# Closing the other rows between the last expert's matmuls, with its down projection in unsplit fp32

## The chip, the cores and the metric

The kernel runs on one core of a Trainium2 chip. The metric is the device time of one execution in microseconds (us). The engines are TensorE (PE; its weight loads are PEld), VectorE (DVE), ScalarE (ACT), GpSimd (POOL) and SyncE (SP); DMA queues carry data between HBM and the on-chip memory.

## What is computed

One layer of a hybrid attention and recurrence backbone. Only its last part matters here, the expert-choice mixture of 16 experts over 1024 tokens of width 1024, each expert taking 128 tokens, and the norm and gated residual after it:

```python
aff = softmax(einsum("btd,de->bte", h, w_router))
top_aff, top_idx = top_k(swapaxes(aff, 1, 2), cap)            # cap = 128
xin = h[top_idx]
g = einsum("becd,edf->becf", xin, w_gate)
u = einsum("becd,edf->becf", xin, w_up)
y = einsum("becf,efd->becd", silu(g) * u, w_down) * top_aff[..., None]
f_lat = zeros((t, d)).at[idx].add(y)
x_lat = x_lat + gt2 * rmsnorm(f_lat, norm_post_ffn)
```

All arrays are fp32.

## The kernel before

Experts run one after the other. Each has 24 weight pieces of 128 x 1024 fp32 (512 KB): 16 for gate and up (two halves of 512 columns, four pieces each of gate and up in turn) and 8 for the down projection, one for each block of 128 hidden features. The pieces are loaded by SyncE (`fetch_to`, lines 1211 to 1221) into a ring of 36 buffers (`ring`, line 1186), far ahead. Two pieces ahead of use (`LEAD`, `take`, lines 1652 to 1657) each is split (`split_piece`, line 1391): ScalarE casts it to a rounded high part (line 1395), VectorE subtracts to get the low part (line 1396). Each product is then three matmuls in the rounded format: high by high, low by high, high by low (lines 1545 to 1547 and 1634 to 1636). The activations are transposed on TensorE and split in the same way (`split_T`, line 1521).

`gate_up` (line 1534) makes one half of the hidden features: 48 matmuls into two accumulators, then tanh on ScalarE and two products on VectorE (lines 1549 to 1551). `hid_T` (line 1554) transposes that half. `down` (line 1625) runs 48 matmuls into `y`. Experts 0 to 14 scale `y` and add it by a GpSimd scatter into `fd` (line 1643), a buffer in HBM that holds the sum over experts.

`out` already holds the residual rows. After expert 14, `bulk` (line 1565) loads the gain row `g2` and the eight 128-row blocks of `fd` into ring buffers, and gathers the last expert's own rows of `fd` and of the residual (line 1578). The closure that it returns, run after the last expert's matmuls (line 1639), closes the rows: a square with a row sum for each block on ScalarE (line 1586), a root for each pair of blocks (`rstd_of`, line 103: one VectorE instruction, line 105, and one GpSimd power, line 106), a scaling by root and gain on VectorE (line 1594), and a store by GpSimd's DMA queue that adds into `out` (line 1595). `fixup` (line 1607) then adds the last expert's `y` to its gathered rows, takes their norm and overwrites those rows of `out` by a scatter (line 1620), which has to come after the eight adding stores.

Instructions go out in each engine's order. For the last expert (`MAN = 1`, line 1673) the order on TensorE, VectorE, ScalarE and GpSimd is that of the program text; before it a planner orders them, and it always orders SyncE's loads. `bulk()` itself is called after expert 14's down projection, still under the planner.

## Time and profile before

| | us |
|---|---|
| median of 3 runs | 1549.85 (1548.72 to 1551.9) |
| the profiled execution | 1549.72 |
| its span in the trace | 1547.8 |
| TensorE busy in it | 1451.9 (94%) |
| VectorE busy | 1165.9 (75%) |
| ScalarE busy | 880.5 (57%) |
| GpSimd busy | 128.8 (8%) |

Times in the views count from the start of the span. Busy time is time in which an engine executes; a stretch in which TensorE is idle is seen in the timeline or in the windows. A matmul's recorded duration runs to its modelled end, so matmuls that follow each other overlap in the records, and the distance between starts tells their pace. A row of the timeline merges like instructions (x2, x3), with the idle time before it and what ended that.

### The profile page before, as it was taken

How to read it: one execution, taken by the hardware profiler on the slowest of the kernel's cores; microseconds unless marked ns; L12 is line 12 of the kernel's file. 1: busy time of each engine (PE TensorE's matmuls, PEld its weight loads, DVE VectorE, ACT ScalarE, POOL GpSimd, SP SyncE). 2: the span in 40 equal slices, each digit the busy share in tenths (PEclk: the TensorE clock that was granted, in tenths of full speed). 3: DMA queues.
4: the chain of work that ended last, by engine and by line, in shares of the span. 5: the costliest groups of instructions: out<-in, count | busy, mean ns of one | idle time of the engine just before them, and what ended most of it. 6: DMA issues, size and time to landing. Idle time of an engine off the chain costs nothing. (4 is left out here: it accounts for less than half of the span.)

```text
span 1547.8 us, 23432 instructions
## 1 busy us (share of the span) xinstructions
PE 1451.9 (94%) x8905; PEld 1198.4 (77%) x8905; DVE 1165.9 (75%) x1588; ACT 880.5 (57%) x1350; POOL 128.8 (8%) x139
## 2 busy tenths in 40 slices
PE   5999999999999988999999979999999999999990
PEld 1988988888978777999978736888888888888870
DVE  2628472849177768999945587999999999999983
ACT  2733443444211117988843315888888888888881
POOL 2100000000000001111000000111111111100003
PEclk9999999999999998999999999999999999999995
DMA  9210010111156616335036886999999999999836
GB/s 337 83 55 29 28 28 28 29 32 39 30 176 194 180 51 167 78 75 150 27 123 243 278 313 233 379 378 383 383 383 372 384 385 384 385 383 383 315 122 149
DMA packets 159308, 316.28 MB, mean 204 GB/s; under 512 B 13790, under 2 KB 50870, under 8 KB 159196
## 3 DMA queue, kind: packets, MB, share of 16 engines
q1 hardware_dynamic: 148592, 277.99, 49.8%
q0 software_dynamic: 9408, 33.54, 9.2%
q10 hardware_dynamic: 1196, 3.26, 0.6%
q8 instruction: 70, 1.15, 0.3%
q14 instruction: 42, 0.34, 0.1%
HBM read 274.36 MB, written 29.38 MB: 196 GB/s over the span
## 5 line engine op out<-in xcount | busy, mean ns | idle before, releaser
L1396 DVE TENSOR_TENSOR mlo<-mraw,mhi 128x1024 fp32r<-128x1024 f32 x340 | 407.5, 1222 | 18.1 <-ACT mhi L1395 13.8
L1395 ACT CAST mhi<-mraw 128x1024 fp32r<-128x1024 f32 x340 | 356.8, 1051 | 79.7 <-PE g L1546 28.2
L166 PE MATMUL pp<-h_hi,whi 128*128 128x512 f32 (+1 forms) x480 | 180.0, 375 | 0.0
L167 PE MATMUL pp<-h_lo,whi 128*128 128x512 f32 (+1 forms) x480 | 178.3, 371 | 0.0
L168 PE MATMUL pp<-h_hi,wlo 128*128 128x512 f32 (+1 forms) x480 | 178.0, 371 | 0.0
L150 ACT CAST whi<-wraw 128x512 fp32r<-128x512 f32 x64 | 39.6, 621 | 121.8 <-PE pp L167 51.8
L881 DVE TENSOR_REDUCE sm<-s 128x1 f32<-128x1280 f32 x64 | 95.3, 1491 | 14.2 <-PE s L876 11.8
L166 PEld LDWEIGHTS pp<-h_hi,whi 128*128 128x128 f32 x480 | 90.4, 188 | 17.7 <-ACT T L478 0.9
L1635 PE MATMUL my<-mhi,hlo 128*128 128x512 f32 x256 | 104.0, 406 | 0.0
L168 PEld LDWEIGHTS pp<-h_hi,wlo 128*128 128x128 f32 x480 | 90.4, 188 | 17.1 <-issue 1.7
L1545 PE MATMUL g<-mhi,xhi 128*128 128x512 f32 x256 | 102.3, 399 | 0.5 <-ACT xhi L1525 0.5
L167 PEld LDWEIGHTS pp<-h_lo,whi 128*128 128x128 f32 x480 | 90.5, 189 | 15.5 <-issue 0.9
L1634 PE MATMUL my<-mhi,hhi 128*128 128x512 f32 x256 | 102.0, 398 | 0.0
L1636 PE MATMUL my<-mlo,hhi 128*128 128x512 f32 x256 | 101.5, 396 | 0.0
L1547 PE MATMUL g<-mlo,xhi 128*128 128x512 f32 x256 | 101.2, 395 | 0.2
L1546 PE MATMUL g<-mhi,xlo 128*128 128x512 f32 x256 | 101.1, 395 | 0.0
L1545 PE MATMUL u<-mhi,xhi 128*128 128x512 f32 x256 | 101.0, 394 | 0.0
L1547 PE MATMUL u<-mlo,xhi 128*128 128x512 f32 x256 | 100.9, 394 | 0.0
L1546 PE MATMUL u<-mhi,xlo 128*128 128x512 f32 x256 | 100.7, 393 | 0.0
L185 PE MATMUL pp<-whi,h_hi 128*128 128x256 f32 x320 | 93.3, 291 | 2.0 <-ACT h_hi L651 2.0
L343 DVE TENSOR_TENSOR X<-X,T 128x640 f32<-128x640 f32 (+1 forms) x112 | 78.2, 760 | 20.4 <-ACT KM L321 12.8
L186 PE MATMUL pp<-whi,h_lo 128*128 128x256 f32 x320 | 92.2, 288 | 0.7 <-DVE h_lo L652 0.7
(326 smaller groups left out, 3148.0 us busy)
## 6 DMA issues: line engine op xcount, KB each, us to landing
mraw<-in_w_down_dram SPq DMA_DIRECT2D x128, 512.0 KB
mraw<-in_w_gate_dram SPq DMA_DIRECT2D x106, 512.0 KB
mraw<-in_w_up_dram SPq DMA_DIRECT2D x106, 512.0 KB
wraw<-in_w_in_dram SPq DMA_DIRECT2D x32, 512.0 KB
aw<-in_w_ada_dram SPq DMA_DIRECT2D x64, 256.0 KB
T<-in_w_gate_dram SPq DMA_DIRECT2D x22, 512.0 KB
T<-in_w_up_dram SPq DMA_DIRECT2D x22, 512.0 KB
aw<-in_w_ada_dram SPq DMA_DIRECT2D x16, 512.0 KB
```

What stands on the lines that cost most here:

```text
L166: nc.tensor.matmul(pp[:, :n], whi, hh, start=(k == 0), stop=False)
L167: nc.tensor.matmul(pp[:, :n], whi, hl, start=False, stop=False)
L168: nc.tensor.matmul(pp[:, :n], wlo, hh, start=False, stop=(k == KT - 1))
L881: nc.vector.tensor_reduce(self.sm[:, m:m + 1], s, axis=AX.X, op=OP.max, negate=True)
L1395: nc.scalar.copy(hi, r)
L1396: nc.vector.tensor_sub(lo, r, hi)
L1545: nc.tensor.matmul(o, x.hi[:, k, :], hi[:, kk, :], start=(k == 0), stop=False)
L1546: nc.tensor.matmul(o, x.lo[:, k, :], hi[:, kk, :], start=False, stop=False)
L1547: nc.tensor.matmul(o, x.hi[:, k, :], lo[:, kk, :], start=False, stop=(k == 7))
L1634: nc.tensor.matmul(y[:, ns], x.hh[:, k, :], hi[:, ns], start=(k == 0), stop=False)
L1635: nc.tensor.matmul(y[:, ns], x.hl[:, k, :], hi[:, ns], start=False, stop=False)
L1636: nc.tensor.matmul(y[:, ns], x.hh[:, k, :], lo[:, ns], start=False, stop=(k == 7))
```

## The change

In the last expert alone:

- The down weights come in another shape: for each half of 512 output columns, four pieces of two feature blocks. They are not split. The hidden half is copied unrounded after its transposes into a ring buffer `x.h`, and the down projection is 16 matmuls with fp32 operands, all eight of the first column half and then all eight of the second.
- `bulk` becomes the class `Rows`, set up at the start of the last expert, inside the stretch with the program's order. Its gathers (residual first, then `fd`) thereby stand on GpSimd ahead of everything else of that expert. The squares write into a ring buffer `junk`.
- Squares 0 to 2 go ahead of the last quarter of the second gate and up half; the other squares, the roots, closes and stores go between the eight groups of two fp32 matmuls, by the table `between` in `last_down`.
- The last expert's own rows are finished by halves (`last_half`): the first half between matmuls, the second after them; then root, residual and scatter as before.

```diff
--- before.py
+++ after.py
@@ -1204,7 +1204,7 @@
     use = []
     for e in range(NE):
         use += [(e, w, hf, p) for hf in range(2) for p in range(4) for w in range(2)]
-        use += [(e, 2, 0, k) for k in range(8)]
+        use += [(e, 2, n, p) for n in range(2) for p in range(4)] if e == NE - 1 else [(e, 2, 0, k) for k in range(8)]
     at = {u: i for i, u in enumerate(use)}
     fetched, raws = [0], {}
 
@@ -1212,9 +1212,9 @@
         while fetched[0] < min(n, len(use)):
             e, w, hf, p = u = use[fetched[0]]
             r = ring()
-            if w < 2:
+            if w < 2 or e == NE - 1:
                 r = r.rearrange("p (k f) -> p k f", k=2)
-                nc.sync.dma_start(r, (wg, wu)[w][e][:, 2 * p:2 * p + 2, hf * 512:(hf + 1) * 512])
+                nc.sync.dma_start(r, (wg, wu, wd)[w][e][:, 2 * p:2 * p + 2, hf * 512:(hf + 1) * 512])
             else:
                 nc.sync.dma_start(r, wd[e][:, p, :])
             raws[u] = r
@@ -1531,13 +1531,13 @@
             x_tiles(x)
         split_T(x.xg[:, g * 512:(g + 1) * 512], x.hi[:, 4 * g:4 * g + 4, :], x.lo[:, 4 * g:4 * g + 4, :])
 
-    def gate_up(e, hf, between=None):
+    def gate_up(e, hf, between={}):
         x = ex[e]
         g = mops.tile([128, 512], F32, name="g", bufs=2)
         u = mops.tile([128, 512], F32, name="u", bufs=2)
         for p in range(4):
-            if p == 2 and between:
-                between()
+            if p in between:
+                between[p]()
             for o, jj in ((g, 0), (u, 1)):
                 hi, lo = take((e, jj, hf, p))
                 for kk in range(2):
@@ -1553,74 +1553,89 @@
 
     def hid_T(e, hf):
         x = ex[e]
+        if e == NE - 1:
+            if hf == 0:
+                x.h = ring().rearrange("p (k t) -> p k t", k=8)
+            tr = mops.tile([128, 4, 128], F32, name="tr", tag="tr")
+            for j in range(4):
+                nc.tensor.transpose(tr[:, j, :], x.hid[hf][:, j * 128:(j + 1) * 128], ident)
+            nc.scalar.copy(x.h[:, 4 * hf:4 * hf + 4, :], tr)
+            return
         if hf == 0:
             x.hh = mo.tile([128, 8, 128], F32R, name="hhi")
             x.hl = mo.tile([128, 8, 128], F32R, name="hlo")
         split_T(x.hid[hf], x.hh[:, 4 * hf:4 * hf + 4, :], x.hl[:, 4 * hf:4 * hf + 4, :])
 
 
-    g2t = []
+
     out2 = out.rearrange("o t d -> (o t) d")
 
-    def bulk():
-        fts, sts = [], []
-        r = modrow[3:4, :]
-        g2 = mo.tile([128, D], F32, name="g2", tag="xg")
-        g2t.append(g2)
-        nc.sync.dma_start(g2, bass.AP(tensor=r.tensor, offset=r.offset, ap=[[0, 128], [1, D]]))
-        for i in range(8):
-            r = ring()
-            nc.sync.dma_start(r, fd[i * 128:(i + 1) * 128, :])
-            fts.append(r)
+    class Rows:
+
+
+        def __init__(self):
+            r = modrow[3:4, :]
+            self.g2 = mo.tile([128, D], F32, name="g2", tag="xg")
+            nc.sync.dma_start(self.g2, bass.AP(tensor=r.tensor, offset=r.offset, ap=[[0, 128], [1, D]]))
+            self.f, self.st = [], []
+            for i in range(8):
+                r = ring()
+                nc.sync.dma_start(r, fd[i * 128:(i + 1) * 128, :])
+                self.f.append(r)
+            x = ex[NE - 1]
+            x.f, x.x1, self.junk = ring(), ring(), ring()
+            for t_, src in ((x.x1, x1d), (x.f, fd)):
+                nc.gpsimd.indirect_dma_start(out=t_, out_offset=None, in_=src[:, :],
+                                             in_offset=bass.IndirectOffsetOnAxis(ap=x.idx[:, 0:1], axis=0))
+
+        def square(self, j):
+            i, z = divmod(j, 2)
+            if z == 0:
+                self.st.append(mo.tile([128, 4], F32, name="fst", bufs=4))
+            nc.scalar.activation(self.junk, self.f[j], AF.Square, accum_out=self.st[i][:, z:z + 1])
+
+        def root(self, i):
+            rstd_of(self.st[i][:, 2:4], self.st[i][:, 0:2], D, 2)
+
+        def close(self, j):
+            i, z = divmod(j, 2)
+            ft = self.f[j]
+            nc.vector.scalar_tensor_tensor(ft, ft, self.st[i][:, 2 + z:3 + z], self.g2, op0=OP.mult, op1=OP.mult)
+            nc.gpsimd.dma_start(out2[j * 128:(j + 1) * 128, :], ft, accum_op=OP.add)
+
+    def last_half(rows, y, o, st, n):
         x = ex[NE - 1]
-        x.f, x.x1 = ring(), ring()
-        for t_, src in ((x.f, fd), (x.x1, x1d)):
-            nc.gpsimd.indirect_dma_start(out=t_, out_offset=None, in_=src[:, :],
-                                         in_offset=bass.IndirectOffsetOnAxis(ap=x.idx[:, 0:1], axis=0))
-
-        def square(i):
-            st = mo.tile([128, 4], F32, name="fst", bufs=4)
-            sts.append(st)
-            for z in range(2):
-                sq = mo.tile([128, D], BF, name="fsq", tag="xhi")
-                nc.scalar.activation(sq, fts[2 * i + z], AF.Square, accum_out=st[:, z:z + 1])
-
-        def root(i):
-            rstd_of(sts[i][:, 2:4], sts[i][:, 0:2], D, 2)
-
-        def close(i):
-            for z in range(2):
-                ft = fts[2 * i + z]
-                nc.vector.scalar_tensor_tensor(ft, ft, sts[i][:, 2 + z:3 + z], g2, op0=OP.mult, op1=OP.mult)
-                nc.gpsimd.dma_start(out2[(2 * i + z) * 128:(2 * i + z + 1) * 128, :], ft, accum_op=OP.add)
-
-        def go():
-            for i in range(4):
-                square(i)
-            root(0)
-            for i in range(4):
-                if i < 3:
-                    root(i + 1)
-                close(i)
-        return go
-
-    def fixup(e, y, o, scale):
+        ns = slice(n * 512, (n + 1) * 512)
+        nc.vector.scalar_tensor_tensor(x.f[:, ns], y[:, ns], x.aff, x.f[:, ns], op0=OP.mult, op1=OP.add)
+        nc.scalar.activation(rows.junk[:, ns], x.f[:, ns], AF.Square, accum_out=st[:, n:n + 1])
+        nc.vector.tensor_mul(o[:, ns], x.f[:, ns], rows.g2[:, ns])
+
+    def last_down(e, rows):
+
+
         x = ex[e]
-        st = mo.tile([128, 4], F32, name="xst", bufs=2)
-        g2 = g2t[0]
-        sq = mo.tile([128, D], BF, name="fsq", tag="xhi")
+        y = mops.tile([128, D], F32, name="my")
+        ys = mo.tile([128, D], F32, name="ys")
+        st = mo.tile([128, 4], F32, name="xst")
+        sq, root, close = rows.square, rows.root, rows.close
+        between = [[(root, 0), (sq, 3)], [(close, 0), (root, 1), (close, 1)], [(hid_T, e, 1), (sq, 4), (sq, 5), (close, 2)],
+                   [(root, 2), (close, 3), (sq, 6)], [(close, 4), (sq, 7)], [(root, 3), (close, 5)],
+                   [(last_half, rows, y, ys, st, 0), (close, 6)], [(close, 7)]]
         for n in range(2):
             ns = slice(n * 512, (n + 1) * 512)
-            nc.vector.scalar_tensor_tensor(x.f[:, ns], y[:, ns], scale, x.f[:, ns], op0=OP.mult, op1=OP.add)
-            nc.scalar.activation(sq[:, ns], x.f[:, ns], AF.Square, accum_out=st[:, n:n + 1])
-            nc.vector.tensor_mul(o[:, ns], x.f[:, ns], g2[:, ns])
+            for p in range(4):
+                for f, *args in between[4 * n + p]:
+                    f(*args)
+                w = raws[e, 2, n, p]
+                for kk in range(2):
+                    k = 2 * p + kk
+                    nc.tensor.matmul(y[:, ns], x.h[:, k, :], w[:, kk, :], start=(k == 0), stop=(k == 7))
+        last_half(rows, y, ys, st, 1)
         nc.vector.tensor_add(st[:, 2:3], st[:, 0:1], st[:, 1:2])
         rstd_of(st[:, 3:4], st[:, 2:3], D, 1)
-        nc.vector.scalar_tensor_tensor(o, o, st[:, 3:4], x.x1, op0=OP.mult, op1=OP.add)
+        nc.vector.scalar_tensor_tensor(ys, ys, st[:, 3:4], x.x1, op0=OP.mult, op1=OP.add)
         nc.gpsimd.indirect_dma_start(out=out2, out_offset=bass.IndirectOffsetOnAxis(ap=x.idx[:, 0:1], axis=0),
-                                     in_=o, in_offset=None)
-
-    close = None
+                                     in_=ys, in_offset=None)
 
     def down(e, between):
         x = ex[e]
@@ -1635,10 +1650,6 @@
                 nc.tensor.matmul(y[:, ns], x.hl[:, k, :], hi[:, ns], start=False, stop=False)
                 nc.tensor.matmul(y[:, ns], x.hh[:, k, :], lo[:, ns], start=False, stop=(k == 7))
         ys = mo.tile([128, D], F32, name="ys")
-        if e == NE - 1:
-            close()
-            fixup(e, y, ys, x.aff)
-            return
         nc.scalar.activation(ys, y, AF.Copy, scale=x.aff)
         nc.gpsimd.indirect_dma_start(out=fd[:, :], out_offset=bass.IndirectOffsetOnAxis(ap=x.idx[:, 0:1], axis=0),
                                      in_=ys, in_offset=None, compute_op=OP.add)
@@ -1651,7 +1662,7 @@
 
     def take(u):
 
-        while made[0] <= min(at[u] + LEAD, len(use) - 1):
+        while made[0] <= min(at[u] + LEAD, len(use) - 9):
             make()
         fetch_to(at[u] + AHEAD)
         return pieces[u]
@@ -1673,11 +1684,16 @@
         if e == NE - MAN:
             ms = tc.manual_schedule(engines={nc.tensor.engine, nc.vector.engine, nc.scalar.engine, nc.gpsimd.engine})
             ms.__enter__()
+            rows = Rows()
+            gate_up(e, 0)
+            gate_up(e, 1, {2: lambda: hid_T(e, 0), 3: lambda: [rows.square(j) for j in range(3)]})
+            last_down(e, rows)
+            break
         counts = pick(e + 2) if e + 2 < NE else None
         gate_up(e, 0)
         if counts:
             counts()
-        gate_up(e, 1, lambda: hid_T(e, 0))
+        gate_up(e, 1, {2: lambda: hid_T(e, 0)})
         between = {2: lambda: hid_T(e, 1)}
         if e + 1 < NE:
             x_T(e + 1, 0)
@@ -1685,8 +1701,6 @@
         if e + 2 < NE:
             between[5] = lambda: gather(e + 2)
         down(e, between)
-        if e == NE - 2:
-            close = bulk()
     ms.__exit__(None, None, None)
     mops_st.close()
     mo_st.close()
```

## Rows read from the trace of the kernel before

**Rows 1.** The page: two groups (busy us, mean ns, idle before).

```profile
L1396 DVE TENSOR_TENSOR mlo<-mraw,mhi 128x1024 fp32r<-128x1024 f32 x340 | 407.5, 1222 | 18.1 <-ACT mhi L1395 13.8
...
L1395 ACT CAST mhi<-mraw 128x1024 fp32r<-128x1024 f32 x340 | 356.8, 1051 | 79.7 <-PE g L1546 28.2
```

**Rows 2.** The chain that ended last, near its end (start, us, what).

```profile
1522.31 15.06 DMA out_dram<-mraw
```

**Rows 3.** Timeline of the end (start, us, engine, line, operation, idle before).

```profile
1523.31 0.75 DVE L1614 SCALAR_TENSOR_TENSOR mraw<-my,ax,mraw 128x512 f32<-128x512 f32 x1
...
1525.89 1.28 DVE L1619 SCALAR_TENSOR_TENSOR ys<-ys,xst,mraw 128x1024 f32<-128x1024 f32 x1 [0.69 <-POOL xst L106]
...
1538.35 1.09 POOL L1620 DMA_INDIRECT out_dram<-ys,idx  x1 [12.49 <-DMA out_dram<-mraw]
```

**Rows 4.** Timeline, 1508 to 1512 us, VectorE and GpSimd.

```profile
1508.73 2.48 DVE L1594 SCALAR_TENSOR_TENSOR mraw<-mraw,fst,g 128x1024 f32<-128x1024 f32 x2
...
1508.86 1.71 POOL L106 TENSOR_TENSOR fst<-fst,half_neg 128x2 f32<-128x2 f32 x1 [1.64 <-DVE fst L105]
...
1510.52 0.95 POOL L1595 DMA_DIRECT2D out_dram<-mraw  x1
...
1511.78 1.61 POOL L1578 DMA_INDIRECT mraw<-fd,idx  x1 [0.31 <-issue]
```

**Rows 5.** Windows: us, busy by engine, granted clock, DMA share, GB/s.

```profile
1485.00:1490.00 5.00, 4.95 (x24) 3.73 (x23) 4.90 (x6) 3.15 (x3) 0.00 (x0) 1.00 1.02 412
...
1490.00:1495.00 5.00, 5.00 (x24) 4.08 (x23) 4.41 (x5) 4.42 (x5) 0.00 (x0) 1.00 0.28 114
...
1530.00:1535.00 5.00, 0.00 (x0) 0.00 (x0) 0.00 (x0) 0.00 (x0) 0.00 (x0) 0.50 1.07 211
```

**Rows 6.** Single lines: count, min/median/max ns, first and last start.

```profile
L1586 ACT ACTIVATE fsq<-mraw x8: 1052/1057/1057, 1503.9 to 1512.1; 128x1024 bf16<-128x1024 f32 x8
...
L1595 POOL DMA_DIRECT2D out_dram<-mraw x8: 844/1176/2073, 1510.5 to 1522.3; - x8
...
DMA to landing us min/median/max: 5.1/11.2/15.1
...
L106 POOL TENSOR_TENSOR fst<-fst,half_neg x4: 724/1424/2314, 1506.5 to 1517.2; 128x2 f32<-128x2 f32 x4
...
L105 DVE TENSOR_SCALAR fst<-fst x4: 159/165/170, 1506.2 to 1513.6; 128x2 f32<-128x2 f32 x4
```

**Rows 7.** Timeline of the last expert, 1490 to 1507 us.

```profile
1490.64 3.12 ACT L1395 CAST mhi<-mraw 128x1024 fp32r<-128x1024 f32 x3
...
1495.07 0.59 ACT L1549 ACTIVATE T<-g 128x512 f32<-128x512 f32 x1
...
1495.53 0.39 PE L1634 MATMUL my<-mhi,hhi 128*128 128x512 f32 x1
...
1497.13 0.69 DVE L1551 SCALAR_TENSOR_TENSOR T<-T,u 128x512 f32<-128x512 f32 x1
...
1498.34 0.60 PE L1524 MATMUL tr<-ident,T 128*128 128x128 f32 x4
...
1498.97 0.59 ACT L1525 CAST hhi<-tr 128x512 fp32r<-128x512 f32 x1 [1.02 <-PE tr L1524]
...
1506.94 0.40 PE L1636 MATMUL my<-mlo,hhi 128*128 128x512 f32 x1
```

**Rows 8.** Line 748, then the timeline: fp32 matmuls elsewhere.

```profile
L748 PE MATMUL mp<-acc,onesc x16: 590/590/591, 450.7 to 548.6; 128*1 128x512 f32 x16
...
450.73 1.02 PE L748 MATMUL mp<-acc,onesc 128*1 128x512 f32 x2 [2.06 <-DVE acc L742]
...
706.01 2.40 PE L907 MATMUL o<-T,aT 128*128 128x128 f32 x20
```

**Rows 9.** Timeline: expert 14's scatter (GpSimd), the row loads (SyncE).

```profile
1473.67 1.57 POOL L1643 DMA_INDIRECT fd<-ys,idx  x1 [32.92 <-ACT ys L1642]
...
1479.77 3.99 SPq L1573 DMA_DIRECT2D mraw<-fd  x8
```

## Prediction

> **What bounds the kernel now.** I read four views, from the outside in: the page, the chain that ended last, the timeline of the last 60 us, and the windows over it. The page says that TensorE carries the kernel and that every weight piece costs 1.05 us of ScalarE (cast) and 1.22 us of VectorE (subtract) [rows 1]. But the chain shows that the end is not TensorE's: 15.06 us of it is one wait, for the last of the eight stores that add the closed rows into the output, issued at 1522.31 and landed at 1537.4 [rows 2]. The reader is to see three things in the timeline [rows 3]: the last expert's own rows are finished on VectorE at 1525.89 + 1.29 = 1527.2; the scatter that writes them starts only at 1538.35, because it overwrites rows that the eight stores add to; and from there to the end of the span are 1547.8 - 1538.35 = 9.45 us that the change doesn't touch. The eight stores begin at 1510.52 [rows 4], after TensorE's last matmul, and in mid-tail the DMA runs full at 211 GB/s with every engine idle (1530:1535 [rows 5]). So the last 40 us are: squares, roots and closes start late, then 27 us of stores. One store is 512 KB, 0.524 MB / 211 GB/s = 2.5 us; the first takes 5.1 us from issue to landing [rows 6].
>
> **Part 1: splits that go away.** The eight down pieces of the last expert are no longer split: 8 x 1.05 = 8.4 us of ScalarE and 8 x 1.22 = 9.8 us of VectorE [rows 1]. Before, these splits fill both engines from about 1492.7 to 1504, which is why the first square starts only at 1503.9 [rows 6, 7]. This is the cover that the moved work takes.
>
> **Part 2: TensorE's down phase.** Before: 48 matmuls from 1495.53 to 1507.3 with four transposes among them, 0.235 us each [rows 7]. After: 16 fp32 matmuls of 512 columns. What an fp32 matmul costs is to be seen elsewhere in this trace: one of 512 columns is two instructions, which together last 1.02 us where one alone has 0.59, so they follow each other at 0.43 us; and with a full 128x128 stationary tile, 20 instructions of 128 columns take 2.40 us, at most 0.12 each, or 0.48 for four times the columns [rows 8]. I take 0.43 (same column count); 32 x 0.43 = 13.8 us, upper end 15.4. One new wait: the second half's transposes now stand right ahead of the matmuls that need them. ScalarE's copy starts 0.63 us after the four transposes do and lasts 0.59 [rows 7]; of these 1.22 the transposes fill 0.4, so TensorE stands about 0.8 us. ScalarE has only squares queued behind that copy. TensorE then ends at 1495.5 + 13.8 + 0.4 + 0.8 = 1510.5 instead of 1507.3: 3.2 us later, and hidden, as the sum shows.
>
> **Part 3: the closing work moves up.** On ScalarE the last two splits that remain end at 1490.64 + 2 x 1.04 = 1492.7 [rows 7]. Three squares follow at 1.18 us (8.2 us for seven starts [rows 6]): 1496.3. The tanh of the second half, queued behind them, so starts at 1496.3 instead of 1495.07; with its 0.59 and VectorE's two products at 0.69 [rows 7], the hidden half is ready at about 1498.4. TensorE asks for it after four fp32 matmuls, at 1495.5 + 3.4 = 1498.9, so the 1.2 us of delay costs nothing, with 0.5 to spare; were the cover gone it would add to TensorE's end one for one, which still has room. VectorE then does root 0 (0.17, and 0.72 on GpSimd at its shortest [rows 6]), 1499.4 with the hand-overs, and the first close, 1.28 (1.24 from start to start [rows 4]): the first store is issued at about 1500.8 instead of 1510.5. The other closes follow it at about 1.3 to 2.0 us (a close of 1.28; every second one has a root before it), so the last store is issued at about 1513.5. That is faster than the 2.5 us a store takes, so from the second store on the DMA sets the pace.
>
> **Part 4: what else moves.** The two gathers of the last expert's rows, now issued among the stores (the first at 1511.78 [rows 4], the second behind it), go to GpSimd's queue right behind the scatter of expert 14. One waits there until that scatter has landed, about 1479.8, when SyncE starts the row loads that wait for the same thing [rows 9]; behind it on GpSimd is nothing until the root at 1498.6. So 2 x 0.5 MB leaves the stores' stretch, where it takes 2.5 us at 412 GB/s (from the window 1485:1490 [rows 5]), and joins the row loads. These have all landed soon after 1490 and then the DMA is nearly still (0.28 over 1490:1495 [rows 5]); 1.3 us more is covered, because only the first three rows are asked for at 1492.7 to 1495. SyncE's own order stays. The last down weights are fetched in pieces of two half rows; the same shape as the gate pieces, and loaded long before. Finishing the last rows: the first half is done between matmuls; of the second, counted from the row at 1523.31 to 1527.2, 3.9 us remain. VectorE is free of closes at about 1513, so the rows are ready near 1517.5, well ahead of the stores.
>
> **The sum.** Last landing before: 1537.4. After: 1500.8 + 5.1 + 7 x 2.5 = 1523.4. By the same formula before gives 1510.5 + 22.6 = 1533.1; the 4.3 left are the gathers (2.5) and 1.8 in which the queue ran thin while GpSimd waited for roots. I take the formula, 14.0 us less, because stores are now issued ahead of need; if the 1.8 stays it is 12.2. The profiled execution is 1549.72 us with a span of 1547.8; the median of the runs is 1549.85. 1549.85 - 14.0 = **1535.9**.
>
> **A rule that speaks against it.** The second root's GpSimd instruction took 1.71 where the first took 0.72; it lies beside a close on VectorE that began 0.13 before it [rows 4, 6]. So roots stretch beside closes. The Trainium skill, "SBUF — State Buffer", section "Who interferes with whom", says why: a VectorE instruction with two SBUF inputs and a GpSimd instruction that reads SBUF exclude each other, and the later one waits. By that rule the three remaining roots would each wait for a close; the trace agrees, with 1.0 us as the wait. In the sum this is the difference between 1.3 and 2.0 us per store, still under 2.5.
>
> **The rivals.** (a) *GpSimd sets the pace.* Every issue takes the longest row (2.07) and every root too (2.31) [rows 6]: from 1500.8, 8 x 2.07 + 3 x 2.31 = 23.5, so the last store is issued by 1524.3, and lands 5.1 - 1 later at about 1528.4: 5 us worse than forecast, 1540.9. For it: VectorE is dense there. Against: the median issue is 1.18, and before, from the first issue at 1510.52 to the last at 1522.31 [rows 2, 4], seven issues, two gathers and two roots fitted into 11.8 us. (b) *TensorE sets the end.* If an fp32 instruction with full weights took twice 0.43, the matmuls would end at 1495.5 + 27.5 + 1.2 = 1524.2, the rows at 1528.1, and the time would be 1528.3 + 9.45 + 1.9 = 1539.7. It decides from about 0.73 us per instruction. Against it: [rows 8]. (c) *The closes don't start early*, because something in the order holds them until TensorE ends at 1510.5; then only the gathers and the thin queue are saved, 4.3 us at most, less 0.4: 1545.9. Nothing on ScalarE, VectorE or GpSimd is seen to wait for that. (d) *Slower: the stores no longer overlap.* Before, they were queued deep; issued one by one, each might pay the 5.1 us of a store alone. 8 x 5.1 = 40.8, last landing 1541.6, time 1554.0. It turns the sign from (1537.4 - 1500.8) / 8 = 4.6 us per store on. Against: the issues come every 1.3 to 2.0 us, under 5.1, so there are always several in the queue.
>
> **How the numbers follow.** Forecast 0.80, (a) 0.08, (b) 0.04, (c) 0.04, (d) 0.03, other 0.01. The forecast's own spread: 1533.5 (runs reach 1.1 below the median, and the first store could be 1 us earlier) to 1539.5 (the 1.8 stays, runs reach 2 above). With (a) and (b) in, 1533 to 1541. A measurement here can tell about 0.2%, 3 us, from no change. Faster by more than that: forecast, (a), (b), half of (c), 0.94; within: half of (c) and the rest, 0.03; slower: (d), 0.03.
>
> **What would show it.** After: the first add into the output is issued near 1500.8; VectorE and ScalarE work on closes while TensorE is busy until about 1510.5; fp32 matmuls follow at 0.43; the gathers are issued before 1482; the last landing is near 1523.4, the scatter about 1 us later. Wrong would be: a first store later than 1503, a DMA stretch after it with less than 200 GB/s, or a scatter that waits for VectorE and not for the stores.

## The result, and the profile after

| | before | after |
|---|---|---|
| median of 4 runs | 1549.73 us (1548.72 to 1551.90) | 1535.56 us (1533.79 to 1538.75) |
| ratio, 95% interval | | 0.9912 (0.9894 to 0.9929) |
| the profiled execution, its span | 1549.72, 1547.8 | 1533.79, 1532.0 |
| TensorE, VectorE, ScalarE busy | 1451.9, 1165.9, 880.5 | 1451.2, 1155.3, 871.8 |

The ratio is the changed kernel's time over that of the kernel before, each time from runs of both in one set. The changed kernel is 14.2 us faster, where 14.0 was forecast. Timed twice more, in the sets of the experiments, it was 1538.81 (ratio 0.9930, 0.9917 to 0.9943) and 1539.25 (0.9923, 0.9908 to 0.9938), which is 10.9 and 11.6 us faster. So the change is worth about 11 to 13 us, and the first median lies a little low. For its profiled execution, the fastest of the four, it is shown below that the rest is not the change.

The timeline of TensorE at the start of the last expert's down phase, in the changed kernel (same columns as [rows 7]):

```profile
1492.22 0.39 PE L1547 MATMUL u<-mlo,xhi 128*128 128x512 f32 x1
1492.45 3.60 PE L1632 MATMUL my<-mraw 128*128 128x512 f32 x8
1495.88 0.60 PE L1561 MATMUL tr<-ident,T 128*128 128x128 f32 x4
1497.15 7.13 PE L1632 MATMUL my<-mraw 128*128 128x512 f32 x16 [0.68 <-ACT mraw L1562]
1505.73 3.70 PE L1632 MATMUL my<-mraw 128*128 128x512 f32 x8 [1.45 <-DVE mraw L1609]
```

The first row is the last gate and up matmul. Its start is the zero point, G, from which all kernels are compared here, since what lies ahead of it varies by some microseconds from run to run. G is 1495.30 before (the first down matmul at 1495.53 of [rows 7], less one start-to-start distance) and 1492.22 after. The fp32 instructions follow each other at 3.43 / 8 = 0.43 us. There are two waits, the predicted one for ScalarE's copy (0.68) and one of 1.45 that the prediction did not have.

GpSimd's timeline, same execution:

```profile
1470.58 1.58 POOL L1654 DMA_INDIRECT fd<-ys,idx  x1 [32.91 <-ACT ys L1653]
1472.47 2.04 POOL L1588 DMA_INDIRECT mraw<-x1d,idx  x1 [0.30 <-issue]
1477.36 0.97 POOL L1588 DMA_INDIRECT mraw<-fd,idx  x1 [2.85 <-DVE mlo L1396]
1495.13 0.73 POOL L106 TENSOR_TENSOR fst<-fst,half_neg 128x2 f32<-128x2 f32 x1 [16.80 <-DVE fst L105]
1497.48 0.99 POOL L1604 DMA_DIRECT2D out_dram<-mraw  x1 [1.62 <-DVE fst L105]
1498.17 1.06 POOL L106 TENSOR_TENSOR fst<-fst,half_neg 128x2 f32<-128x2 f32 x1
...
1509.09 0.84 POOL L1604 DMA_DIRECT2D out_dram<-mraw  x1 [0.33 <-DVE mraw L1603]
1511.45 0.57 POOL L106 TENSOR_TENSOR xst<-xst,half_neg 128x1 f32<-128x1 f32 x1 [1.51 <-DVE xst L105]
1522.55 1.09 POOL L1637 DMA_INDIRECT out_dram<-ys,idx  x1 [10.53 <-DMA out_dram<-mraw]
```

Expert 14's scatter, the two gathers right behind it, then roots and adding stores from 1497.48 to 1509.09, and the last scatter, which waits for the stores and not for VectorE. The chain of waits ends like that of before ([rows 2]), with a shorter wait:

```profile
1509.09 12.47 DMA out_dram<-mraw
```

VectorE's last instruction for the last expert's rows lies 9 us ahead of that scatter:

```profile
1512.05 1.28 DVE L1636 SCALAR_TENSOR_TENSOR ys<-ys,xst,mraw 128x1024 f32<-128x1024 f32 x1 [0.69 <-POOL xst L106]
```

And the windows over the stores' stretch (columns as in [rows 5]):

```profile
1500.00:1505.00 5.00, 4.29 (x10) 1.54 (x9) 4.35 (x7) 1.66 (x4) 3.50 (x6) 1.00 1.08 200
1505.00:1510.00 5.00, 3.70 (x8) 1.44 (x8) 4.29 (x6) 0.72 (x2) 3.19 (x4) 1.00 1.03 188
1510.00:1515.00 5.00, 0.00 (x0) 0.00 (x0) 2.51 (x5) 0.72 (x2) 0.57 (x1) 0.79 1.07 211
1515.00:1520.00 5.00, 0.00 (x0) 0.00 (x0) 0.00 (x0) 0.00 (x0) 0.00 (x0) 0.50 1.03 205
```

The DMA share is full throughout, at 188 to 211 GB/s, and now lies beside TensorE's and VectorE's work for the first 10 us. Counted from G (the column "before" is from the one profile of that kernel):

| us after G | before | forecast | after |
|---|---|---|---|
| first adding store issued | 15.2 | 5.5 | 5.3 |
| last adding store issued | 27.0 | 18.2 | 16.9 |
| TensorE's last matmul ends | 12.0 | 15.2 | 17.2 |
| last expert's rows ready | 31.9 | 22.2 | 21.1 |
| last store landed | 42.1 | 28.1 | 29.3 |
| last scatter starts | 43.1 | 29.1 | 30.3 |
| end of the span | 52.5 | 38.5 | 39.8 |

**Where the other 3 us come from.** By this table the change gives 52.5 - 39.8 = 12.7 us. The two spans differ by 15.8. The remaining 3.1 are there already when expert 0 scatters, hundreds of microseconds ahead of the first instruction that differs. GpSimd's timelines of before, after and after once more (the run named after_again below):

```profile
977.95 2.13 POOL L1643 DMA_INDIRECT fd<-ys,idx  x1 [5.35 <-ACT ys L1642]
```
```profile
974.88 2.12 POOL L1654 DMA_INDIRECT fd<-ys,idx  x1 [5.35 <-ACT ys L1653]
```
```profile
980.12 2.11 POOL L1654 DMA_INDIRECT fd<-ys,idx  x1 [5.35 <-ACT ys L1653]
```

The windows 935 to 945 us of the same three show TensorE's granted clock (the column ahead of the last two) at 0.89, 1.00 and 0.81 of its 2.4 GHz:

```profile
935.00:945.00 10.00, 9.01 (x52) 6.01 (x50) 6.52 (x14) 4.03 (x5) 1.25 (x1) 0.89 0.16 52
```
```profile
935.00:945.00 10.00, 9.05 (x47) 7.12 (x48) 9.18 (x16) 6.22 (x7) 1.25 (x1) 1.00 0.39 110
```
```profile
935.00:945.00 10.00, 9.01 (x48) 5.12 (x47) 5.68 (x17) 2.23 (x3) 1.25 (x1) 0.81 0.00 1
```

The same kernel is thus 5.2 us apart from itself at that point, and the order of the three clocks is that of the three scatters. What starts that difference was not looked for.

### The profile page after: what moved, and what is told of

Read it like the earlier page. It is cut to its first block, busy times and chain, and to the rows that moved or that the text cites. A ratio compares the mean times of both kernels' runs of the same rounds, so it can differ in the third digit from the quotient of the medians.

```text
span 1532.0 us, 23371 instructions
## 1 busy us (share of the span) xinstructions
PE 1451.2 (95%) x8889; PEld 1193.5 (78%) x8889; DVE 1155.3 (75%) x1578; ACT 871.8 (57%) x1342; POOL 127.5 (8%) x139
## 5 line engine op out<-in xcount | busy, mean ns | idle before, releaser
L1396 DVE TENSOR_TENSOR mlo<-mraw,mhi 128x1024 fp32r<-128x1024 f32 x332 | 398.2, 1223 | 19.1 <-ACT mhi L1395 15.0
L1395 ACT CAST mhi<-mraw 128x1024 fp32r<-128x1024 f32 x332 | 348.4, 1051 | 78.7 <-PE g L1546 28.8
L881 DVE TENSOR_REDUCE sm<-s 128x1 f32<-128x1280 f32 x64 | 95.3, 1491 | 13.1 <-PE s L876 10.7
L1650 PE MATMUL my<-mhi,hlo 128*128 128x512 f32 x240 | 97.7, 407 | 0.0
L1649 PE MATMUL my<-mhi,hhi 128*128 128x512 f32 x240 | 95.6, 398 | 0.0
L1651 PE MATMUL my<-mlo,hhi 128*128 128x512 f32 x240 | 95.2, 396 | 0.0
```

Source lines behind the costliest of these rows:

```text
L881: nc.vector.tensor_reduce(self.sm[:, m:m + 1], s, axis=AX.X, op=OP.max, negate=True)
L1395: nc.scalar.copy(hi, r)
L1396: nc.vector.tensor_sub(lo, r, hi)
L1649: nc.tensor.matmul(y[:, ns], x.hh[:, k, :], hi[:, ns], start=(k == 0), stop=False)
L1650: nc.tensor.matmul(y[:, ns], x.hl[:, k, :], hi[:, ns], start=False, stop=False)
L1651: nc.tensor.matmul(y[:, ns], x.hh[:, k, :], lo[:, ns], start=False, stop=(k == 7))
```

## The experiments

The theory: the end is set by eight adding stores, which are paced by the DMA from the first one on, so that the gain is the earlier first store plus the gathers that left their stretch. Against it stand three rivals: one half of the change alone brings the whole gain, TensorE's later end and its new wait already take part of the gain, or GpSimd's issues set the pace. Each experiment starts from the changed kernel. A diff shows the experiment's edit against it.

### The changed kernel again: after_again and after_third

No edit.

> The changed kernel as it is, beside the others. In its first profile, from the end of the last gate and up matmul (1492.45) the first adding store is issued 5.0 us later, the last one lands 29.1 later, and the span ends 39.55 later; in the kernel before that last distance is 1547.8 - 1495.53 = 52.3. Theory: these distances repeat within 0.7 us, and the 3.1 us by which the first profile reaches that point earlier than the kernel before don't repeat, since nothing ahead of the last expert has changed. Rival: the 3.1 us belong to the change and repeat. Time by the theory: the kernel before less 12.7 us, a ratio near 0.992; by the rival less 15.8, 0.990.

> The changed kernel as it is, on the chip of the two runs beside it. Theory: the last gate and up matmul to the end of the span takes 39.6 within 0.7 us again, 12.9 less than in the kernel before; ratio 0.992 to 0.993. Rival (the gain differs from chip to chip): outside 0.990 to 0.995.

Measured 1538.81 and 1539.25. In their profiled executions the first store is issued 5.26 and 5.27 us after G, the last one lands at 29.0 and 30.3, and the span ends at 39.4 and 40.7, against 39.8 in the first profile. The gain counted from G is thus 11.8 to 13.1 us, and the rival, that the 3.1 us belong to the change, is out: the second profile is 5.2 us behind the first at expert 0 and gains as much from G. The wait of 1.45 us in TensorE is there each time. The part that the change touches repeats within 1.3 us; within 0.7 of the first profile was expected, and the third lies 0.9 from it. The first store is issued at the same distance from G in all three, so what differs lies between its issue and the last landing (the store stretch, below).

### One half of the change at a time

Both kernels keep the gathers where the change puts them.

**The order of before, with the unsplit weights.** All squares, roots, closes and both finishing halves stand behind the last matmul:

```diff
-        between = [[(root, 0), (sq, 3)], [(close, 0), (root, 1), (close, 1)], [(hid_T, e, 1), (sq, 4), (sq, 5), (close, 2)],
...
+        between = [[], [], [(hid_T, e, 1)], [], [], [], [], []]
...
+        for j in range(8):
+            sq(j)
+        root(0)
...
+        last_half(rows, y, ys, st, 0)
```

> Unsplit fp32 down projection as in the change, but squares, roots, closes and stores stand in the program after the last matmuls, in the order of the kernel before (all squares, then two roots, closes by pairs, then both halves of the last rows). Theory (the stores set the end, so it moves with the first store): with no splits left, ScalarE can begin the squares right behind the copy of the second transposes, about 1.5 us earlier than now for the tanh and 4.2 later for the first square; two pairs of squares must be done before the first close, so the first store is issued about 10 us after the last gate and up matmul instead of 5.0, and the end comes 5 us later than in the changed kernel, still 8 us ahead of the kernel before. Rival (it is the removed splits alone that count, the place of the closes doesn't): within 1.5 us of the changed kernel. Second rival (the interleaving is all of it): within 3 us of the kernel before.

**The interleaved order, with the split kept.** The last down weights are split again and multiplied three times:

```diff
-                w = raws[e, 2, n, p]
+                hi, lo = take((e, 2, n, p))
...
-                    nc.tensor.matmul(y[:, ns], x.h[:, k, :], w[:, kk, :], start=(k == 0), stop=(k == 7))
+                    nc.tensor.matmul(y[:, ns], x.hh[:, k, :], hi[:, kk, :], start=(k == 0), stop=False)
+                    nc.tensor.matmul(y[:, ns], x.hl[:, k, :], hi[:, kk, :], start=False, stop=False)
+                    nc.tensor.matmul(y[:, ns], x.hh[:, k, :], lo[:, kk, :], start=False, stop=(k == 7))
```

> The closes stand between the matmuls as in the change, but the down weights are still split and each product is three matmuls in the rounded format, by the same column halves. Theory: ScalarE gets 8 x 1.05 and VectorE 8 x 1.22 us of splits back, queued among squares and closes. VectorE then has some 2.5 us of work per store, as much as a store takes, and TensorE waits for splits behind closes. The first store is issued 1 to 2 us later (two splits ahead of it), the last lands 2 to 6 us later, and the last rows are finished late because TensorE ends late: 4 to 8 us slower than the changed kernel, still faster than the kernel before. Rival (the place of the closes is all of it): within 1.5 us of the changed kernel.

The first gave 1544.31 (0.9968, 0.9956 to 0.9980), the second 1542.11 (0.9947, 0.9934 to 0.9960), both beside 1538.81 for the whole; the first is 5.5 us slower than that, where 5 were expected. The first store is issued 11.4 and 8.9 us after G, the last one lands at 36.4 and 34.2. With the split kept VectorE spaces the issues of the stores: its timeline has splits between the closes,

```profile
1512.97 1.22 DVE L1396 TENSOR_TENSOR mlo<-mraw,mhi 128x1024 fp32r<-128x1024 f32 x1
1514.11 1.28 DVE L1603 SCALAR_TENSOR_TENSOR mraw<-mraw,fst,g 128x1024 f32<-128x1024 f32 x1
1515.31 1.22 DVE L1396 TENSOR_TENSOR mlo<-mraw,mhi 128x1024 fp32r<-128x1024 f32 x1
```

and the last store goes out only at 1523.01, 25.2 after G, with a wait of 8.96 behind it:

```profile
1523.01 8.96 DMA out_dram<-mraw
```

Even so the first store does most of it: it is issued 3.6 us later than in the changed kernel (1 to 2 were expected), the last one lands 4.8 us later. By the medians this kernel is 3.3 us slower than the changed one, by the profile 4.8, where 4 to 8 were expected.

So neither half gives the whole gain alone: 5.4 and 7.6 us of 10.9, each with what the moved gathers give. Both bring the first store forward, to 11.4 and 8.9 us after G from 15.2, and only together to 5.3. That the earliest closes need VectorE's and ScalarE's time that the splits took is as parts 1 and 3 of the prediction had it.

### Do the stores set the end, and how much room is behind them?

**Four stores instead of eight.** The rows of blocks 4 to 7 are closed and not written:

```diff
-            nc.gpsimd.dma_start(out2[j * 128:(j + 1) * 128, :], ft, accum_op=OP.add)
+            if j < 4:
+                nc.gpsimd.dma_start(out2[j * 128:(j + 1) * 128, :], ft, accum_op=OP.add)
```

> The changed kernel without four of its eight adding stores (the second half of the 1024 rows isn't written; squares, roots and closes stay). Distances are from the start of the last gate and up matmul. Theory (stores set the pace at 2.5 us each): the last of four lands 4 x 2.5 = 10 us earlier than the last of eight, at about +19; then the last expert's own rows, ready at +21.1, set the end, and the span ends near +30.8 instead of +39.5: 8.7 us faster than the changed kernel. Rival (the stores overlap and only the issue of the last one counts, fixed latency behind it): the fourth is issued at +10.1, lands 12.4 later at +22.5, the end is at +33, 6.5 us faster. Second rival (something else holds the scatter): no change.

**Plain stores instead of adding ones.** The stores overwrite the residual rows:

```diff
-            nc.gpsimd.dma_start(out2[j * 128:(j + 1) * 128, :], ft, accum_op=OP.add)
+            nc.gpsimd.dma_start(out2[j * 128:(j + 1) * 128, :], ft)
```

> The changed kernel with its eight stores as plain writes instead of adds (the residual rows are overwritten, not added to). Theory (the adding is what makes a store take 2.5 us of the full DMA): a plain store of 0.52 MB goes at the 400 GB/s and more of the row loads, 1.3 us, less than the 1.2 to 2.3 us between issues; the last lands about 4 us after its issue, at +21 from the last gate and up matmul; the own rows are ready at +21.1 and set the end, near +31: 8.5 us faster than the changed kernel. Rival (the issue on GpSimd or the writing direction sets 2.5 us): no change.

**32 more fp32 instructions on TensorE**, ahead of the last two of the eight groups:

```diff
+                if n == 1 and p == 3:
+                    pad = mops.tile([128, 512], F32, name="g", bufs=2)
+                    for k in range(16):
+                        nc.tensor.matmul(pad, x.h[:, k % 8, :], raws[e, 2, 1, 3][:, k % 2, :], start=True, stop=True)
```

> The changed kernel with 16 more fp32 matmuls of 512 columns into an unused accumulator, ahead of its last four. Theory: 32 instructions at 0.43 are 13.8 us more of TensorE; between the finished rows (+21.1 from the last gate and up matmul) and the scatter (+30.2) are 9.1 us of slack, so the end comes 13.8 - 9.1 = 4.7 us later. Rival (TensorE's down phase is on the path): 13.8 us later. Rival (the fp32 instructions take twice 0.43 with full weights): 18.5 us later.

Four stores: 1528.28 (0.9857, 0.9842 to 0.9872). Plain stores: 1529.70 (0.9861, 0.9844 to 0.9877). From G the spans end at 30.5 and 30.6, where near 31 was expected for both. In all three the last scatter waits for VectorE and no longer for the DMA. Its row in GpSimd's timeline, with four stores, with plain stores, and with more matmuls:

```profile
1518.71 1.09 POOL L1638 DMA_INDIRECT out_dram<-ys,idx  x1 [1.61 <-DVE ys L1637]
```
```profile
1520.03 1.06 POOL L1637 DMA_INDIRECT out_dram<-ys,idx  x1 [1.61 <-DVE ys L1636]
```
```profile
1526.97 1.09 POOL L1641 DMA_INDIRECT out_dram<-ys,idx  x1 [1.61 <-DVE ys L1640]
```

So with the stores out of the way the floor is about 9 us below the changed kernel, and two edits that share nothing but the shorter stores give the same floor. A plain store lands 2.9 to 3.1 us after its issue, while the adding ones of the changed kernel take 5.2 (the first) to 12.5 (the last). The window 1505 to 1510 of that profile, which begins 0.9 us after its first store's issue, shows 320 GB/s, though plain stores go out only every 1.2 to 2.3 us; in the changed kernel no window of the stretch is above 212. In the trace, a packet of 4 KB takes 0.16 us (median) in a plain store and 0.33 in an adding one.

The added matmuls take 13.9 us of TensorE,

```profile
1507.17 13.90 PE L1630 MATMUL g<-mraw 128*128 128x512 f32 x32
```

and the span ends at 44.6 from G instead of 39.4 to 40.7: 4 to 5 us later, 4.7 expected. The median is 1541.49 (0.9945, 0.9931 to 0.9958), some 2.5 us above the two later medians of the changed kernel, which are from other sets; the profiled execution, 1538.22, was the lowest of its set. The rivals' 13.8 and 18.5 us are far off. Of 13.9 us 9 or more cost nothing. This is the room of the own rows, from the other side.

### TensorE's unpredicted wait: y in two tiles

```diff
-        y = mops.tile([128, D], F32, name="my")
+        y = [mops.tile([128, 512], F32, name="g", bufs=2) for n in range(2)]
```

> The two column halves of the last product stand in two accumulator tiles of their own instead of one. In the changed kernel's trace TensorE stands 1.45 us ahead of the second half's last eight matmuls and waits for VectorE's read of the first half, which lies in other columns of the same tile. Theory: with two tiles this wait is gone, TensorE ends 1.4 us earlier, and the time stays the same within 1 us, since the stores set the end. Rival (TensorE and the last rows set the end): 1.4 us faster.

The wait is gone; the 24 matmuls behind the copy run in one piece:

```profile
1502.88 10.57 PE L1632 MATMUL g<-mraw 128*128 128x512 f32 x24 [0.68 <-ACT mraw L1562]
```

So the wait came from one tile holding both column halves: VectorE's read of the finished half held back TensorE's writes of the other. (With all of VectorE's reads behind the last matmul, in the order of before, it isn't there either.) TensorE ends 15.5 after G, close to the 15.2 forecast, but the time is 1539.05 (0.9926, 0.9911 to 0.9941) and the end 40.15 from G: no change. The stores hide it.

### The gathers among the stores

```diff
-        between = [[(root, 0), (sq, 3)], [(close, 0), (root, 1), (close, 1)], [(hid_T, e, 1), (sq, 4), (sq, 5), (close, 2)],
+        between = [[(root, 0), (sq, 3)], [(close, 0), (rows.gather,), (root, 1), (close, 1)], [(hid_T, e, 1), (sq, 4), (sq, 5), (close, 2)],
```

> The changed kernel with its two gathers put back to where they were before, on GpSimd behind the first adding store. Theory: 1.05 MB more on the full queue at about 410 GB/s, 2.5 us later landing of the last store, 2.5 us slower than the changed kernel, if the second store isn't held up; GpSimd's two issues of 1 to 2 us each also delay the second store, which can add 1 us. Rival (the gathers fill the stretch in which the queue runs thin): no change.

Measured 1539.30 (0.9933, 0.9920 to 0.9947). The changed kernel's own ratios are 0.9912, 0.9923 and 0.9930, so by the medians the gathers cost 0.5 to 3.3 us, with intervals of 2 us on either side: neither nothing nor 2.5 us is ruled out. In the profile the gathers are issued at 1502.46 and 1503.81, the second store 2.8 us later than without them, and the end is at 42.9 from G, 2.2 to 3.5 us later than in the three profiles of the changed kernel. TensorE waits 4.08 us there for VectorE, which waits for the gathered rows; this too is hidden. The second store lands 6.6 us after the first, against 2.7 to 3.0 in the changed kernel, and from the third on the landings are 2.5 to 2.6 apart. So the one profile agrees with the prediction's 2.5 us, and the medians can't tell.

### Going on: the second gate and up half unsplit as well

With the theory so far, everything that lets the first store go out earlier pays, up to the 9 us of room. The three versions multiply the last expert's second gate and up half in fp32 too (16 fp32 products instead of 48, no splits), and move squares, roots and closes into it. Its `x.t` is the unrounded transposed input:

```diff
+                if e == NE - 1 and hf == 1:
+                    for kk in range(2):
+                        k = 2 * p + kk
+                        nc.tensor.matmul(o, x.t[:, k, :], raws[e, jj, hf, p][:, kk, :], start=(k == 0), stop=(k == 7))
+                    continue
```

They differ in who makes `x.t`: in v1 a further ScalarE copy from the transposes, in v2 one copy from which the split is then made, in v3 one GpSimd add of the two split parts, in the last expert's stretch:

```diff
+            x.t = ring().rearrange("p (k t) -> p k t", k=8)
+            nc.gpsimd.tensor_add(x.t, x.hi, x.lo)
```

> A further step: the last expert's second gate and up half takes its weights in fp32 unsplit too (x is copied unrounded beside its split), the closes move up into that half, and y stands in two accumulator tiles. Theory: TensorE pays 32 x 0.43 - 48 x 0.233 = 2.6 us there, ScalarE and VectorE lose eight more splits each, and the first store waits only for the loads of its rows, 10 to 12 us earlier than in the changed kernel. The stores then share the DMA with the row loads; loads, gathers and stores together are 4.2 + 1.05 MB at 410 GB/s and 8 x 2.5 us, 33 us from about 1481 on, 1514 by the changed kernel's clock. TensorE ends near +15.5 + 2.6 and the last rows are ready 3.9 later, +22 or 1514.5. So the scatter starts near 1515 instead of 1522.5: 7 us faster than the changed kernel. Rival (row loads and stores slow each other by more than their bytes): 2 to 4 us faster. Rival (an early store into the output delays the loads of the rows behind it, and squares, closes and the last tanh wait in turn): no faster.

> The further step with two things mended. In its first form ScalarE's additional copy of x held the transposes' accumulator, TensorE stood 1.4 and 0.7 us for it in expert 14's down projection and its granted clock then fell for a while: from expert 13's scatter to expert 14's took 40.1 us instead of 35.3. Now the unsplit copy comes first and the split is made from it. And the last square, which waited for its row to 1506, no longer stands ahead of the last tanh. Theory: 4.8 and 0.8 us less, so 5 us faster than the first form, near 1529 and 9 to 10 us faster than the changed kernel. Rival (the rows' loads set the end, and they start with expert 14's scatter, so the last store lands no earlier against that scatter): 4.8 us less at most, and TensorE's 0.8 shows nowhere.

> As the second version with the second half's rows unsplit, but x.t of the last expert comes from one add of x.hi and x.lo on GpSimd in the last expert's stretch, so that ScalarE gets no additional copy while expert 14 runs. Theory (the additional copy held TensorE up ahead of expert 14's scatter): the distance from the scatter of expert 13 to that of expert 14 goes back from 39.8 us to 35.0 to 35.3 us, the distance from expert 14's scatter to the end stays near 52.3 us, and the time falls by about 4.5 us to some 1526 to 1527 us, a ratio near 0.984. Rival: the add (128 x 1024 fp32 on GpSimd, beside VectorE's splits) delays the last expert's first matmuls or the gathers, so that the distance from expert 14's scatter to the end grows by what the other distance gives back, and the time stays near 1531 us, a ratio near 0.987.

| | median, ratio | scatter of expert 13 to that of 14 | from there to the end |
|---|---|---|---|
| changed kernel (third) | 1539.25, 0.9923 | 34.5 | 62.4 |
| v1 | 1534.12, 0.9899 (0.9885 to 0.9913) | 40.1 | 52.9 |
| v2 | 1530.85, 0.9868 (0.9853 to 0.9883) | 39.8 | 52.3 |
| v3 | 1533.47, 0.9886 (0.9869 to 0.9904) | 34.6 | 59.0 |

All three beat the changed kernel: v2 by 8.4 us in the same set (9 to 10 were expected), v1 and v3 by 5 to 6 us against its medians from other sets (for v1, 7 were expected). In v1 and v2 the additional copies, made while expert 14 runs, delay TensorE there. Of v2:

```profile
1467.79 0.66 PE L1524 MATMUL tr<-ident,T 128*128 128x128 f32 x4 [1.39 <-ACT mraw L1526]
1469.12 0.50 PE L1658 MATMUL my<-mhi,hhi 128*128 128x512 f32 x1 [0.67 <-ACT hhi L1528]
```

With a third wait of 0.23 these are 2.3 us. Behind them the granted clock is lower (0.66 in the window 1470 to 1475), and eight matmul distances take 3.4 us where they take 1.9 at the full clock. That is 3.8 of the 5.3 us by which expert 14 takes longer than in the changed kernel; the rest is not explained. v2's expectation, that its order would mend v1's stall, did not hold (39.8 for 40.1): v1 has the same waits of 1.39, 0.67 and 0.23. Of the 3.3 us between the two medians, from two sets, the profiles explain 0.9, the two columns' differences; the rest is not explained. v3 has the 5 us back in expert 14, and loses more than that behind it, in the way of its rival: the add lies beside VectorE's splits. First GpSimd, then VectorE (line view of the tile `mlo`, 1471 to 1478), then TensorE:

```profile
1473.02 2.93 POOL L1587 TENSOR_TENSOR mraw<-xhi,xlo 128x1024 f32<-128x1024 f32 x1
```
```profile
L1396 DVE TENSOR_TENSOR mlo<-T,mhi x3: 1210/1226/4360, 1470.0 to 1477.0; 128x1024 fp32r<-128x1024 f32 x3
```
```profile
1477.10 0.80 PE L1552 MATMUL g<-mlo,xhi 128*128 128x512 f32 x1 [3.28 <-DVE mlo L1396]
```

One subtraction takes 4.36 us instead of 1.22: it starts at 1472.68, just ahead of the add, and ends 1.1 us after it. TensorE stands 3.28 us for it. After that idle stretch the granted clock is lower (windows, 0.65 and 0.67 where v2 has 1.00):

```profile
1475.00:1480.00 5.00, 2.90 (x7) 2.33 (x8) 4.45 (x4) 1.05 (x1) 3.81 (x3) 0.65 0.71 139
1480.00:1485.00 5.00, 5.00 (x17) 3.92 (x16) 2.53 (x3) 2.10 (x2) 0.16 (x1) 0.67 1.01 407
```

In these two windows matmuls start every 0.43 us, the pace of 1.2 GHz, instead of 0.23, from 1477.7 to 1483.2: 13 of them, 13 x 0.195 = 2.5 us. With the wait that is 5.8 of the 6.7 us by which v3's tail is longer than v2's. And TensorE now ends the chain: the last scatter waits for VectorE's `ys`. In v2 it does so too (and in v1), but only just: its stores land at 1521.45 and `ys` is ready at 1521.8. That is where an earlier first store stops paying, since stores and own rows now end together. The forecasts of 1526 to 1527 (theory) and near 1531 (rival) both missed the 1533.47; the interval reaches down to the second.

## Why the prediction was right, point by point

**What sets the end: shown.** That the eight adding stores bound the tail ([rows 2, 3]) held before and after; removing half of them or making each cheaper takes 9 us off at once, and making TensorE later by 13.9 costs only 4 to 5.

**The first store: right.** Forecast 5.5 us after G, measured 5.26 to 5.27. The sum of squares, tanh, products, root and close was good to 0.3. With one half of the change alone it is 8.9 or 11.4.

**TensorE's down phase: right in pace, one wait missed.** The 0.43 us from a shape with one column of weights ([rows 8]) held for full weights, and the wait for the copy was 0.68 where 0.8 was said. The 1.45 us wait was in no part: the prediction took the two column halves for independent, and they are parts of one tile. It was covered, as the extra 3.2 us were; rival (b) was far off.

**The store stretch: pace right, late landings let go.** Forecast 5.1 + 7 x 2.5 = 22.6 us from the first issue to the last landing; measured 1521.56 - 1497.48 = 24.1, and 23.7 and 25.0 in the other two profiles. Store by store the trace shows where the excess of 1.1 to 2.4 us lies:

| landing, us after the one before | before | after | after_again | after_third |
|---|---|---|---|---|
| first (after its issue) | 5.1 | 5.2 | 5.4 | 5.4 |
| second | 6.8 | 2.9 | 2.7 | 3.0 |
| third | 2.5 | 3.6 | 3.2 | 4.2 |
| fourth to eighth, each | 2.5 | 2.5 | 2.5 | 2.5 |

So the pace of 2.5 us, taken from a window in which every engine was idle ([rows 5], 211 GB/s), held from the third landing on, and what came in addition is the second and above all the third landing. The windows over these two show 188 to 201 GB/s, and those behind them 205 to 212, in all three profiles. The prediction had named a stretch below 200 GB/s as a sign that it is wrong; this is that sign, and it concerns this term. It is not that busy engines make the pace slower: in v2 the stores land 2.5 us apart from the second one on (the first takes 7.6 us there), also in a window in which TensorE, VectorE and GpSimd are busy for 4.33, 4.39 and 3.76 of 5 us (columns as in [rows 5]):

```profile
1505.00:1510.00 5.00, 4.33 (x14) 1.95 (x13) 4.39 (x5) 0.59 (x1) 3.76 (x4) 1.00 1.06 210
```

Nor is it a late issue: in the first profile the third store was issued 4.7 us ahead of the second's landing. In the trace, the packets of 4 KB that take over 0.45 us instead of 0.33 all lie in the first 11 us behind the first store's issue: 33 to 50 of them in the three profiles, and only two in v2. Why they are slow was not tried and stays open.

The prediction had 1.8 us in excess of its formula before, explained them by a queue that ran thin while GpSimd waited for roots, and let them go because stores would be issued ahead of need. The stores were, and the excess stayed. Before, it lies ahead of the second landing (6.8 less 2.5 for the store and 2.5 for the gathers), and the queue was not thin there (DMA share 1.01):

```profile
1515.00:1520.00 5.00, 0.00 (x0) 0.00 (x0) 2.95 (x3) 0.00 (x0) 5.00 (x7) 0.50 1.01 253
```

12.2 us, which the prediction named for the case that the 1.8 stays, is what the runs show: 11.8 to 13.1 from G, and 10.9 to 14.2 by the medians.

**The gathers: placed right, price open.** They left the stores' stretch (1472.47 and 1477.36). The second waited for VectorE's release of a buffer (2.85 us), which was not foreseen and cost nothing. By the sum from G, the first store 9.9 us earlier and a stretch of 24.1 for 26.9 give the 12.7, and the 2.8 is about what the forecast charged for the gathers (2.5). Put back among the stores, they cost 2 to 3.5 us in one profile; the medians don't settle it.

**Roots beside closes.** Measured 1.06, 1.02 and 1.03 us against 0.73 for the one that runs alone: 0.3 us, not a whole close of 1.28, for the close beside each had only 0.3 to 0.4 us left when the root began. With the order of before (closes in pairs) they are 1.72, 2.12 and 2.75. It never mattered to the end, as forecast. By the Trainium skill, "SBUF — State Buffer", section "Who interferes with whom", a VectorE instruction with two SBUF inputs contends with a GpSimd instruction that reads SBUF. The trace agrees in direction. In v3, where a subtraction on VectorE and an add on GpSimd both read two tiles, the subtraction takes 4.36 us instead of 1.22; the 3.1 more are about the 2.93 of the add. By the records the subtraction had started 0.34 us ahead of the add, so which of the two had to wait for the other isn't shown.

**The rivals.** (a) GpSimd's pace: the last store was issued 16.9 after G, earlier than forecast. (b) is answered above. (c) The closes did start early. (d) The stores did overlap: their landings take 5.2 to 12.5 us, with 1.2 to 2.3 between issues.

**The number.** 1535.9 against 1535.56 is luck in part. A gain that is 1.3 us short of the forecast from G met a set of low times: its profiled execution was 3.1 us ahead at expert 0, and its median lies over 3 us below the two later ones. Those, 1538.8 and 1539.3, are inside the range too, near the end that the prediction had set for the 1.8 that stays.

## What to carry to other kernels

When the end is a queue of stores, ask two things of it: when its first one can be issued, and what the rest cost each. Here freeing the engines that feed the first store and giving them an order that reaches it sooner each brought part of the gain, and both together the whole. Read a stretch of transfers landing by landing and not by its mean: here the mean of 2.7 us was a pace of 2.5 and one or two late landings, and an excess whose explanation was not checked is better kept in the forecast than let go. And compare two executions from a common instruction close ahead of the change: the spans alone would have credited the change with 3 us that were lost or won at expert 0.

## What the runs showed of the hardware

- An adding store of 512 KB lands 5.1 to 5.4 us after issue when first in an empty queue (before and the three profiles of the changed kernel), and the following ones land 2.5 us apart at 211 GB/s, also beside busy engines (v2, 210 GB/s), but for one or two early ones that take 2.7 to 4.2. The same store without the add lands in 2.9 to 3.1 us, eight in a row, and GpSimd issues it in 0.53 to 0.62 us instead of 0.84 to 1.12. Its 4 KB packets take 0.16 us (median), those of the adding store 0.33.
- An fp32 matmul of 512 columns is two instructions of 0.43 us at a granted clock of 1.00, the same for one column of weights ([rows 8]) and for 128. In place of three instructions of 0.23 it costs TensorE 0.16 us per product (two in a piece), and saves 1.05 us of ScalarE and 1.22 of VectorE per weight piece.
- A GpSimd add of 128 x 1024 beside a VectorE subtraction of the same size stretched the latter from 1.22 to 4.36 us. The 3.3 us for which TensorE stood were followed by windows at a granted clock of 0.65 to 0.67.
